# The weight sums of layer 1's modulation and of both gates, moved from the vector engine to GpSimd

## The chip, the cores and the metric

One core of one Trainium2 chip. The metric is the device time of one execution in microseconds (us), the median of the runs of one kernel. The engines are named as in the profile: PE (TensorE), DVE (VectorE), ACT (ScalarE), POOL (GpSimd) and SP (SyncE, which here issues every DMA).

## The reference, cut to what matters

Two layers of a diffusion backbone over 256 latent and 256 context tokens of width 2048. Each layer is modulated by a vector that comes from the conditioning vector `c`:

```python
silu_c = jax.nn.silu(c)
for l in range(DEPTH):
    mod_l = silu_c @ w_mod[l] + b_mod[l]
    sh_l, sc_l, gt_l = jnp.split(mod_l[:, None, :], 3, axis=-1)
    h_lat = rms_norm(x, g_pre[l]) * (1.0 + sc_l) + sh_l
    ...
    x = x + gt_l * rms_norm(y_lat, g_post[l])
```

Layer 0 is differential attention beside a two-way gated linear recurrence (HGRN2); layer 1 is a pooling mixer. `w_mod[l]` is 2048 x 6144 in float32. The change touches the products `silu_c @ w_mod` that make `sh_l` and `sc_l` of layer 1 and the gates `gt_l` of both layers: 16 blocks of 512 output columns, each a sum over 2048 rows.

## The kernel before, in words

Every large matrix product runs in float32r with both factors split in a high and a low part. A weight piece is 256 rows by 512 columns (`load_w`, line 209): one DMA of 512 KB into a tile `w` (4 buffers), ACT rounds it to `hi` (line 217), DVE forms `lo = w - hi` (line 218), and PE multiplies (line 288): 12 products of 128x512 for a group of two token tiles, 24 for a group of four. `Group.weights` (line 269) asks for a piece with raised priority, and `group` (line 433) walks over the 8 pieces of a group.

The 16 blocks of the change are made beside these groups by `gemv_row` (line 336), a generator that a `Filler` steps (line 393; `beside`, line 427, steps it some fraction of a time per piece). A step loads 256 rows of `w_mod` by 512 columns into a tile `wf`, of which there are two buffers (line 340), and adds its two k-tiles of 128 rows to the accumulator `ga` of 128x512, each scaled by a value of `csil` per partition. There are 8 steps to a block, 128 in all. When a block is done, `feature_sink` or `gate_sink` sums `ga` over the 128 partitions with products by ones on PE (lines 363 and 384) and adds bias and gain. Seven blocks are stepped in the first attention batch and the second HGRN2 batch (`hg_batch(1, ..., fills=FH)` with FH = 2, two steps per piece), five in the second attention batch and up to the layer's end, four in layer 1 (lines 1062 to 1063).

The order is set by a scheduler at build time: it simulates the engines, picks by priority, and writes one fixed program per engine. The sums stand with a lowered priority (`FILLB = -400`), their DMAs do not. At run time each engine and each queue goes through its own list in order; a wait holds everything behind it. All loads are in SP's one list, so a load that waits for its buffer holds the loads behind it.

POOL has 35 instructions in the profile before, all at the start or small: `memset`s of one column for the scans of HGRN2 (lines 576 and 579) and of a table `ct` of 48 columns (line 631), which DVE reads next.

Of the kernel before, what the change touches and what calls it, by code (L numbers as in the profile page):

```python
# [31 lines left out]
ALU = mybir.AluOpType  # L32
# [22 lines left out]
def hybrid_kernel(  # L55
# [5 lines left out]
    nc = tc.nc  # L61
# [6 lines left out]
    def alloc(tag, shape, dtype, bufs):  # L68
        return sb.tile(shape, dtype, tag=tag, bufs=bufs, name=f"{tag}_{next(names)}")

    def t2(shape, dtype=F32):
        return alloc("t2", shape, dtype, 4)
# [22 lines left out]
    def log_exp_table(after=None):  # L95
# [15 lines left out]
        out=sel, in_=ident.rearrange("p (a b) -> p b a", b=32)[:, 0:2, :], axis=AX.X)  # L111
# [97 lines left out]
    def load_w(src, k2, col, tag="w", bufs=4):  # L209
        w = alloc(tag, [P, 2, 512], F32, bufs)  # L210
        nc.sync.dma_start(
            out=w, in_=src[k2 * 256:k2 * 256 + 256, col:col + 512].rearrange("(k p) n -> p k n", p=P))
        return w
# [122 lines left out]
    def gemv_row(l, col, sink):  # L336

        acc = alloc("ga", [P, 512], F32, 2)
        for k2 in range(8):
            w = load_w(w_mod[l], k2, col, "wf", 2)  # L340
            with tc.high_priority(offset=FILLB):
                for i in range(2):
                    sc = csil[:, 2 * k2 + i, 0:1]
                    if k2 + i == 0:
                        nc.vector.tensor_scalar(out=acc, in0=w[:, i, :], scalar1=sc, scalar2=None, op0=ALU.mult)
                    else:
                        nc.vector.scalar_tensor_tensor(out=acc, in0=w[:, i, :], scalar=sc, in1=acc, op0=ALU.mult,  # L347
                                                       op1=ALU.add)
            if k2 < 7:
                yield  # L350
        fill.later.append([WAIT, lambda: sink(acc)])
        yield
# [170 lines left out]
    for i, n in ((3, 4), (7, 1)):  # L523
        t = t2([P, n, P])
# [364 lines left out]
    for f in range(4):  # L889
        fill.add(gemv_row(1, 2048 + 512 * f, feature_sink(1, 1, 4 * f, 4)))  # L890
    for f in range(3):
        fill.add(gemv_row(1, 512 * f, feature_sink(1, 0, 4 * f, 4)))
    da_batch(0, BD0, FD0)
    hg_batch(1, bgs=BH, fills=FH)
    for f in range(4):
        fill.add(gemv_row(0, 4096 + 512 * f, gate_sink(0, f)))
# [112 lines left out]
    for f in range(4):  # L1009
        t = alloc("gk", [P, 2, 512], F32, 4)  # L1010
# [54 lines left out]
    for j in range(4):  # L1065
# [12 lines left out]
        t = alloc("y", [P, 2, 512], F32, 4)  # L1078
# [115 lines left out]
```

## Time and profile before

| | |
|---|---|
| time, median of 3 runs | 1260.59 us (1259.58 to 1264.09) |
| the profiled execution's own time | 1258.11 us |
| its span in the profile | 1256.3 us |
| mean granted TensorE clock | 0.996 |
| PE busy | 1200.7 us (96%) |
| DVE busy | 897.4 us (71%) |
| ACT busy | 600.6 us (48%) |
| POOL busy | 4.4 us (0%) |
| HBM read | 260.33 MB, 209 GB/s over the span |

The span runs from the first to the last instruction; the execution's own time has some 2 us around it. Busy shares are means over stages that differ: what a change is worth in a stage is read from that stage's rows. The chain of waits follows the end of the program back from releaser to releaser, so a line in it was, at that moment, what everything else waited for. Line numbers are those of the kernel before; the change has one line less, so that a line below 347 has its number there less one.

### The profile page before, as it was taken

What the parts mean: (1) busy time and instruction counts of PE and PEld (TensorE: products, weight loads), DVE (VectorE), ACT (ScalarE), POOL (GpSimd) and SP (SyncE); (2) the same over time, 40 slices, a digit from 0 to 9 for tenths busy, and PEclk for the clock granted to TensorE, in tenths of its full rate; (3) what the DMA queues carried; (4) which work ended last, traced back from release to release, by engine and by line L of the source; (5) the groups of instructions that cost most, each with busy time, mean ns of one, the idle gap of its engine ahead of it and who ended that gap; (6) DMA issues with size and microseconds to landing.
All of it is one profiled execution on the core that took longest, in us unless ns stands there. A gap on an engine that the chain in (4) does not pass through costs nothing.

```text
span 1256.3 us, 16359 instructions
## 1 busy us (share of the span) xinstructions
PE 1200.7 (96%) x5938; PEld 951.4 (76%) x5938; DVE 897.4 (71%) x1530; ACT 600.6 (48%) x1039; POOL 4.4 (0%) x35
## 2 busy tenths in 40 slices
PE   3999999999999999999999999999999999999997
PEld 2566677778887777887787877787877877888885
DVE  3554559998767676788968697696676776976654
ACT  4231324784445633336544457764565444444452
POOL 0000000000000000000000000000000000000000
PEclk9999999999999999999999999999999999999999
DMA  9988757762453466777535266676656888875553
GB/s 290 333 303 304 264 174 234 222 197 68 137 162 99 126 220 222 250 257 228 161 101 169 84 219 223 195 250 203 218 184 202 311 303 301 268 222 185 184 209 110
DMA packets 144246, 263.52 MB, mean 210 GB/s; under 512 B 8306, under 2 KB 21540, under 8 KB 144164
## 3 DMA queue, kind: packets, MB, share of 16 engines
q1 hardware_dynamic: 144164, 262.46, 63.2%
q8 instruction: 47, 0.77, 0.2%
q14 instruction: 35, 0.29, 0.1%
HBM read 260.33 MB, written 2.10 MB: 209 GB/s over the span
## 4 chain that ended last, share of the span: by engine, by line
PE 59%; DVE 17%; DMA 16%; issue 4%; ACT 2%; SPq 1%; DVEq 0%; ACTq 0%
PE acc L288 41%; DMA wf<-in_w_mod_dram 13%; PE auxb L288 8%; DVE ga L347 5%; DVE lo L218 5%; PE aux L328 2%; PE auxb L733 2%; DMA w<-in_ev_w_in_dram 1%; SPq L128 1%; PE aux L841 1%; ACT hi L217 1%; PE auxb L817 1%; PE aux L363 1%; PE auxb L1103 1%; DVE tb L610 1%
## 5 line engine op out<-in xcount | busy, mean ns | idle before, releaser
L288 PE MATMUL acc<-hi,h 128*128 128x512 f32 x1928 | 623.8, 397 | 3.0 <-ACT h L217 2.0
L217 ACT ACTIVATE hi<-w 128x1024 fp32r<-128x1024 f32 x265 | 280.6, 1059 | 398.4 <-PE acc L288 255.0
L288 PEld LDWEIGHTS acc<-hi,h 128*128 128x128 f32 x1928 | 361.1, 188 | 86.5 <-issue 10.0
L218 DVE TENSOR_TENSOR lo<-w,hi 128x1024 fp32r<-128x1024 f32 x265 | 322.8, 1221 | 139.1 <-ACT hi L217 136.6
L288 PE MATMUL acc<-lo,h 128*128 128x512 f32 x964 | 380.9, 395 | 3.4 <-DVE lo L218 3.3
L347 DVE SCALAR_TENSOR_TENSOR ga<-wf,csil,ga 128x512 f32<-128x512 f32 x240 | 179.5, 748 | 64.0 <-DMA wf<-in_w_mod_dram 60.8
L288 PEld LDWEIGHTS acc<-lo,h 128*128 128x128 f32 x964 | 181.7, 188 | 46.7 <-DVE lo L218 7.6
L288 PE MATMUL acc<-h,hi 128*128 128x512 f32 x512 | 162.0, 397 | 0.0
L288 PEld LDWEIGHTS acc<-h,hi 128*128 128x128 f32 x512 | 95.4, 190 | 18.8 <-ACT qT L560 0.2
L288 PE MATMUL acc<-h,lo 128*128 128x512 f32 x256 | 100.8, 394 | 0.0
L288 PE MATMUL auxb<-h,hi 128*128 128x512 f32 x256 | 82.8, 405 | 0.7 <-ACT hi L217 0.4
L288 PEld LDWEIGHTS auxb<-h,hi 128*128 128x128 f32 x256 | 45.9, 188 | 24.7 <-issue 8.8
L310 DVE TENSOR_TENSOR tb<-auxb,tb 128x512 f32<-128x512 f32 x56 | 38.1, 687 | 25.9 <-PE auxb L288 25.5
L288 PEld LDWEIGHTS acc<-h,lo 128*128 128x128 f32 x256 | 48.4, 189 | 10.2
L288 PE MATMUL auxb<-h,lo 128*128 128x512 f32 x128 | 49.9, 395 | 0.0
L328 PE MATMUL aux<-h,tb 128*32 128x128 f32 (+2 forms) x320 | 29.7, 472 | 9.3 <-DMA h<-in_w_mod_dram 5.4
L218 DVE TENSOR_TENSOR h<-t,h 128x512 fp32r<-128x512 f32 x40 | 27.0, 686 | 5.7 <-ACT h L217 5.6
L819 DVE TENSOR_REDUCE tinyb<-auxb 128x1 f32<-128x512 f32 x32 | 20.7, 684 | 13.7 <-PE auxb L817 13.7
L733 PEld LDWEIGHTS auxb<-tb 128*128 128x128 f32 x192 | 25.3, 191 | 5.5 <-DVE tb L664 2.3
L733 PE MATMUL auxb<-tb 128*128 128x128 f32 x192 | 27.1, 279 | 1.5 <-DVE tb L664 1.5
L217 ACT ACTIVATE h<-t 128x512 fp32r<-128x512 f32 x40 | 24.5, 625 | 6.8 <-DVE t L912 5.0
L288 PEld LDWEIGHTS auxb<-h,lo 128*128 128x128 f32 x128 | 23.9, 188 | 4.9
(248 smaller groups left out, 1181.7 us busy)
## 6 DMA issues: line engine op xcount, KB each, us to landing
w<-in_ev_w_in_dram SPq DMA_DIRECT2D x144, 512.0 KB, 4.3
wf<-in_w_mod_dram SPq DMA_DIRECT2D x132, 512.0 KB, 4.5
w<-in_od_w_in_dram SPq DMA_DIRECT2D x64, 512.0 KB, 4.6
h<-in_w_mod_dram SPq DMA_DIRECT2D x20, 1024.0 KB, 6.9
w<-in_ev_w_out_dram SPq DMA_DIRECT2D x32, 512.0 KB, 3.7
w<-in_od_w_out_dram SPq DMA_DIRECT2D x32, 512.0 KB, 3.5
v<-in_w_mod_dram SPq DMA_DIRECT2D x24, 256.0 KB, 3.5
h<-in_w_mod_dram SPq DMA_DIRECT2D x8, 512.0 KB, 7.1
```

The lines of the kernel that those rows point to most:

```text
L128: nc.sync.dma_start(out=w[:, k:k + m, :], in_=w_mod[l][(kt0 + k) * P:(kt0 + k + m) * P, col:col + n].rearrange("(k p) n -> p k n", p=P))
L217: return (nc.scalar.activation(out=hi, in_=src, func=AF.Copy), nc.vector.tensor_tensor(out=lo, in0=src, in1=hi.bitcast(F32), op=ALU.subtract))
L218: nc.vector.tensor_tensor(out=lo, in0=src, in1=hi.bitcast(F32), op=ALU.subtract))
L288: newest[:] = [nc.tensor.matmul(self.ps[j], a, b, start=self.mm[j] == 1, stop=self.mm[j] == 6 * of)]
L310: nc.vector.tensor_tensor(out=t, in0=ps, in1=t, op=ALU.add)
L328: nc.tensor.matmul(ps[32 * j:32 * j + 32, :], cpad[:, kt, :], w[:, i, :], start=kt < 4, stop=kt >= 12)
L347: nc.vector.scalar_tensor_tensor(out=acc, in0=w[:, i, :], scalar=sc, in1=acc, op0=ALU.mult, op1=ALU.add)
L363: nc.tensor.matmul(pt[:, b, :], ev[:, sl], sel if l == 0 else ones[:, 0:2], start=True, stop=True)
L610: nc.vector.tensor_tensor_scan(out=o, data0=ones[:, 0:n], data1=src, initial=0.0, op0=ALU.mult, op1=ALU.add)
L733: nc.tensor.matmul(pt[:, i, s, :], wk(s * P), wq(s * P), start=True, stop=True)
L817: last = nc.tensor.matmul(ps[m], qT[i][r, h, sl], ks[h][k][r, :], start=n == 0, stop=n == 2)
L819: nc.vector.reduce_max(out=mx[:, m:m + 1], in_=ps[m], axis=AX.X)
```

## The change

For each k-tile, one instruction on DVE (multiply by a scalar and add the accumulator) becomes two on POOL: a multiplication of the loaded tile in place, and an addition to `ga`. The first k-tile of a block is multiplied straight into `ga`.

```diff
             with tc.high_priority(offset=FILLB):
                 for i in range(2):
                     sc = csil[:, 2 * k2 + i, 0:1]
-                    if k2 + i == 0:
-                        nc.vector.tensor_scalar(out=acc, in0=w[:, i, :], scalar1=sc, scalar2=None, op0=ALU.mult)
-                    else:
-                        nc.vector.scalar_tensor_tensor(out=acc, in0=w[:, i, :], scalar=sc, in1=acc, op0=ALU.mult,
-                                                       op1=ALU.add)
+                    t = acc if k2 + i == 0 else w[:, i, :]
+                    nc.gpsimd.tensor_scalar(out=t, in0=w[:, i, :], scalar1=sc, scalar2=None, op0=ALU.mult)
+                    if k2 + i > 0:
+                        nc.gpsimd.tensor_tensor(out=acc, in0=acc, in1=t, op=ALU.add)
```

POOL gets 256 multiplications and 240 additions of 128x512; DVE loses 16 and 240 instructions. The scheduler writes all lists anew.

SP's list in the second HGRN2 batch, before (`w`: a weight piece; `wf`: a step of the sums):

```order
L211 DMA w_4082<-in_ev_w_in_dram 128x2x512
L211 DMA wf_4001<-in_w_mod_dram 128x2x512
L211 DMA wf_4005<-in_w_mod_dram 128x2x512
L211 DMA w_4128<-in_ev_w_in_dram 128x2x512
L211 DMA wf_4054<-in_w_mod_dram 128x2x512
L211 DMA wf_4058<-in_w_mod_dram 128x2x512
L211 DMA w_4166<-in_ev_w_in_dram 128x2x512
```

and with the change:

```order
L211 DMA w_4275<-in_ev_w_in_dram 128x2x512
L211 DMA wf_4221<-in_w_mod_dram 128x2x512
L211 DMA wf_4227<-in_w_mod_dram 128x2x512
L211 DMA wf_4263<-in_w_mod_dram 128x2x512
L211 DMA w_4317<-in_ev_w_in_dram 128x2x512
L211 DMA wf_4269<-in_w_mod_dram 128x2x512
L211 DMA wf_4305<-in_w_mod_dram 128x2x512
L211 DMA w_4365<-in_ev_w_in_dram 128x2x512
```

There are still about two `wf` loads to each weight load, and each weight load still stands behind the `wf` loads ahead of it.

DVE's list at the same place, before:

```order
L347 SCALAR_TENSOR_TENSOR ga_3881<-wf_4054,csil,ga_3881 128x512
L218 TENSOR_TENSOR lo_3953<-w_3950,hi_3952 128x1024
L347 SCALAR_TENSOR_TENSOR ga_3881<-wf_4054,csil,ga_3881 128x512
L347 SCALAR_TENSOR_TENSOR ga_3881<-wf_4058,csil,ga_3881 128x512 x2
L218 TENSOR_TENSOR lo_4012<-w_4009,hi_4011 128x1024
```

and POOL's list there with the change:

```order
L345 TENSOR_SCALAR wf_4616<-wf_4616,csil 128x512 x2
L347 TENSOR_TENSOR ga_4548<-ga_4548,wf_4616 128x512 x2
L345 TENSOR_SCALAR wf_4661<-wf_4661,csil 128x512 x2
L347 TENSOR_TENSOR ga_4548<-ga_4548,wf_4661 128x512 x2
L345 TENSOR_SCALAR wf_4667<-wf_4667,csil 128x512 x2
L575 MEMSET tb_4535 128x1
L347 TENSOR_TENSOR ga_4548<-ga_4548,wf_4667 128x512 x2
```

The sums have left DVE's list, where they stood between the `lo` instructions; on POOL they fill the list, four instructions to a `wf` tile, and the small `memset`s stand among them.

## Rows read from the trace of the kernel before

**Rows 1.** The page, part 1: busy time and share of the span.
```profile
PE 1200.7 (96%) x5938; PEld 951.4 (76%) x5938; DVE 897.4 (71%) x1530; ACT 600.6 (48%) x1039; POOL 4.4 (0%) x35
```
**Rows 2.** The page, part 4: the chain that ended last, by line.
```profile
PE acc L288 41%; DMA wf<-in_w_mod_dram 13%; PE auxb L288 8%; DVE ga L347 5%; DVE lo L218 5%; PE aux L328 2%; PE auxb L733 2%; DMA w<-in_ev_w_in_dram 1%; SPq L128 1%; PE aux L841 1%; ACT hi L217 1%; PE auxb L817 1%; PE aux L363 1%; PE auxb L1103 1%; DVE tb L610 1%
```
**Rows 3.** The page, part 5: costliest groups; busy us, mean ns; idle before, releaser.
```profile
L288 PE MATMUL acc<-hi,h 128*128 128x512 f32 x1928 | 623.8, 397 | 3.0 <-ACT h L217 2.0
...
L218 DVE TENSOR_TENSOR lo<-w,hi 128x1024 fp32r<-128x1024 f32 x265 | 322.8, 1221 | 139.1 <-ACT hi L217 136.6
...
L347 DVE SCALAR_TENSOR_TENSOR ga<-wf,csil,ga 128x512 f32<-128x512 f32 x240 | 179.5, 748 | 64.0 <-DMA wf<-in_w_mod_dram 60.8
```
**Rows 4.** Busy time of each engine in four stretches, granted clock, DMA share, GB/s.
```profile
433.00:582.00 149.00, 143.90 (x684) 117.03 (x683) 111.21 (x175) 51.95 (x100) 0.69 (x7) 0.99 0.71 234
955.00:1057.00 102.00, 99.30 (x433) 78.84 (x432) 75.94 (x90) 44.81 (x50) 0.00 (x0) 1.00 0.87 298
664.00:668.00 4.00, 1.88 (x11) 1.35 (x10) 4.00 (x13) 2.68 (x6) 0.00 (x0) 1.00 0.52 157
668.00:672.00 4.00, 4.00 (x12) 3.13 (x11) 4.00 (x12) 1.93 (x4) 0.00 (x0) 0.57 0.62 202
```
**Rows 5.** Timeline of SP's queue in the second HGRN2 batch: start, us, line.
```profile
484.31 0.37 SPq L211 DMA_DIRECT2D w<-in_ev_w_in_dram  x1
484.98 1.94 SPq L211 DMA_DIRECT2D wf<-in_w_mod_dram  x2
490.97 0.37 SPq L211 DMA_DIRECT2D w<-in_ev_w_in_dram  x1
```
**Rows 6.** Instructions on tile wf, 433 to 582 us: first and last issue, landing.
```profile
L211 SPq DMA_DIRECT2D wf<-in_w_mod_dram x45: 367/368/368, 433.7 to 581.3; - x45
...
DMA to landing us min/median/max: 3.6/4.5/5.5
```
**Rows 7.** The same, 955 to 1057 us.
```profile
L211 SPq DMA_DIRECT2D wf<-in_w_mod_dram x26: 367/461/862, 955.6 to 1056.9; - x26
...
DMA to landing us min/median/max: 3.6/5.3/6.6
```
**Rows 8.** The same, issues alone: 735 to 765, 175 to 218 and 818 to 850 us.
```profile
L211 SPq DMA_DIRECT2D wf<-in_w_mod_dram x8: 367/368/368, 735.2 to 760.4; - x8
...
L211 SPq DMA_DIRECT2D wf<-in_w_mod_dram x10: 367/368/421, 175.7 to 213.7; - x10
...
L211 SPq DMA_DIRECT2D wf<-in_w_mod_dram x6: 367/368/461, 818.8 to 844.7; - x6
```
**Rows 9.** Groups of instructions on POOL, whole span.
```profile
L631 POOL MEMSET ct<- 128x48 f32 x8 | 1.1, 138 | 217.0 <-DVE tb L725 181.8 <-ACT tb L655 35.2
L576 POOL MEMSET tb<- 128x1 f32 x8 | 0.8, 100 | 379.6 <-DVE gk L559 211.6 <-ACT hi L217 140.9 <-PE aux L841 14.5
...
L196 POOL MEMSET tb<- 128x512 f32 x1 | 0.5, 524 | 0.0
...
masks.py:199 POOL TENSOR_SCALAR_AFFINE_SELECT ident<-ident 128x128 f32<-128x128 f32 x1 | 0.3, 292 | 0.0
```
**Rows 10.** The lo instruction on DVE: 433 to 582, 955 to 1057, 735 to 765 us.
```profile
L218 DVE TENSOR_TENSOR lo<-w,hi 128x1024 fp32r<-128x1024 f32 x23 | 28.1, 1220 | 6.4 <-ACT hi L217 6.4
...
L218 DVE TENSOR_TENSOR lo<-w,hi 128x1024 fp32r<-128x1024 f32 x33 | 39.6, 1218 | 0.4 <-ACT hi L217 0.3
...
L218 DVE TENSOR_TENSOR lo<-w,hi 128x1024 fp32r<-128x1024 f32 x8 | 9.7, 1217 | 0.0
```
**Rows 11.** Waits of SP's queue, 433 to 582 us: us in total, times, longest.
```profile
SPq L211 <- DVE lo L218: 50.6, 21, 5.2
SPq L211 <- DVE ga L347: 40.1, 30, 4.2
```
**Rows 12.** The chain in order of time, 640 to 680 us: start, us, what.
```profile
644.51 5.47 PE acc L288 x24
667.95 6.40 PE acc L288 x21
```

## The prediction

> **What bounds the kernel now.** Read first the busy shares: PE is busy 1200.7 of 1256.3 us, POOL not at all, DVE 71% [rows 1]. So the kernel is bound by PE, and all idle time of PE together is some 55 us, much of it at the start: no relief of another engine can give more. Then the chain of waits: it is PE's large product for 41%, but 13% of it are loads of `wf`, and 5% the sums on DVE [rows 2]. This is the sign to notice: a load that feeds a side job is in the chain, since the weight loads stand behind it in SP's one list. The timeline of SP's queue shows the pattern, one weight piece, two `wf`, one weight piece, some 6.7 us apart [rows 5], and SP's waits there name two holders, `lo` (the buffer of a weight piece, 50.6 us) and `ga` (the buffer of a `wf` tile, 40.1 us) [rows 11].
>
> That stage, 433 to 582 us, is the one to work out. 45 `wf` loads are issued in 147.6 us, 3.35 us each, 6.71 us a pair [rows 6]. With two buffers a `wf` buffer goes round in load plus sums: the median load lands 4.5 us after its issue [rows 6], two sums take 2 x 0.75 = 1.5 us [rows 3], in all 6.0, and 0.7 us are left for waiting in DVE's list. So the ring of the two buffers already runs about as fast as it can, and PE, busy 143.9 of 149 us there [rows 4], just keeps up with it.
>
> **The change part by part.**
>
> *DVE loses its sums*: 179.5 us of busy time and 64 us of waiting ahead of them [rows 3]. PE does not wait for DVE's throughput: it has 5.1 us of idle time in the first stage and 2.7 us in 955 to 1057 us [rows 4]. I count the gain as nothing; the cover is PE itself.
>
> *POOL's price for an instruction of 128x512.* No such instruction is in the trace, so it is bounded. A `memset` of 128x512 takes 524 ns, one of 128x1 100 ns: 0.83 ns a column for writing alone [rows 9]. The select on 128x128, which reads and writes one tile, takes 292 ns: (292 - 100) / 128 = 1.5 ns a column [rows 9]. So a multiplication lies between 0.52 and 100 + 512 x 1.5 = 0.87 us. A second input adds at least nothing (0.52) and, by the step from `memset` to select, once more 0.68 ns a column: 100 + 512 x 2.18 = 1.22 us. I take the upper ends, since the select is the only row in which POOL reads: a `wf` tile costs 2 x (0.87 + 1.22) = 4.2 us instead of 1.5. The lower end is 4 x 0.52 = 2.1 us, the middle 3.1.
>
> A page of the Trainium skill has prices for this: GPSIMD Engine Reference, section Performance versus the Vector engine, gives 4497 ns for an addition of 2048 float32 columns, a quarter of which is an estimate of 1.12 us, and its section Engine selection calls one input roughly line-rate, by its clock of 1.2 GHz an estimate of 0.43 us. By these a tile would take 2 x (1.12 + 0.53 with 0.1 us to start) = 3.3 us, and the sum below would come to about 1330 us. No run here shows either yet.
>
> *The second HGRN2 batch.* A buffer goes round in 4.5 + 4.2 + 0.1 for the wake-ups = 8.8 us, 4.4 us a tile; POOL alone would need 4.2. 44 intervals x 4.4 = 194 us instead of 147.6: **+46 us**. PE needs its weight pieces every 5.46 us (24 products of 228 ns, [rows 12]) and gets one in 8.8, as each stands behind two `wf` loads that wait for POOL; four `w` buffers fill once and cannot help a stage of some 22 pieces.
>
> *Layer 1, 955 to 1057 us.* 26 loads in 101.3 us, 4.05 us each, landing after 5.3 us [rows 7]. (5.3 + 4.2 + 0.1) / 2 = 4.8 us; 25 x 4.8 = 120 us: **+19 us**. PE is busy 99.3 of 102 us there [rows 4], so there is no slack to take it.
>
> *The bunches.* Elsewhere `wf` loads come in six bunches of 6 to 10, of which three stand in [rows 8]: 8 in 25.2 us, 10 in 38.0, 6 in 25.9. At 4.4 us they need 30.8, 39.6 and 22: +6, +2 and nothing. **+7 us** in all.
>
> *DVE and POOL side by side.* No row shows both reading SBUF at once. If they do so freely, this costs nothing. If one holds the other off whenever DVE reads two tiles, `lo` alone (28.1 us in the first stage, 39.6 in the second, 9.7 in the densest bunch, [rows 10]) has to find time beside POOL's sums: 45 x 4.2 + 28 = 217 instead of 194 us, 26 x 4.2 + 40 = 149 instead of 120, 34 + 10 = 44 instead of 31, together about 65 us. Nothing in the rows is nearer to either end; I take half, about **+35 us**, and keep 0 and 65.
>
> *POOL's other work.* The one-column `memset`s and the tables [rows 9] now wait in POOL's list behind up to a tile's sums, and DVE's scans, with the `lo` behind them, wait for the `memset`s. In a stage that POOL paces they are covered by its own pace; outside it a wait is up to 4 us for a few of the 24. Not in the sum, up to 15 us in the range.
>
> *PE's clock.* PE will stand still some 3 us between pieces. At 664 to 668 us PE is busy 1.88 of 4 us, and in the next 4 us its granted clock is 0.57, the half level for most of it [rows 4]; 21 products then take 6.40 us where 4.8 is usual [rows 12], 1.6 us lost. In the paced stages 5.5 + 1.6 us is still under 8.8, so this costs nothing there.
>
> *Sum*: 46 + 19 + 7 + 35 = 107 us on the profiled execution's 1258.1 us: 1365 us. That execution was 2.5 us under the median, so I say **1368 us**.
>
> **The rivals.**
>
> *B, the two engines take turns fully.* The mechanism is that of the term of which I took half. It gives 46 + 19 + 7 + 65 = 137 us, 1395 us, and with DVE's other two-input work and the `memset` waits, which then meet a busy POOL everywhere, up to 1450; I put it at 1410. For it: DVE's chain of `lo` is dense just where POOL is. Against it: nothing in the trace. The rule stands in the Trainium skill, SBUF — State Buffer, section Who interferes with whom: a DVE instruction with two SBUF inputs contends with a GpSimd instruction that reads SBUF, and the second waits to the end. No run here has shown it yet.
>
> *C, POOL is cheap.* With the middle price of 3.1 us and no interference the first stage takes 44 x 3.85 = 169 us (+22), the second 25 x 4.25 = 106 (+5): 1285 to 1300 us. For it: writing runs at 0.83 ns a column, and reading may run beside it. Against it: the select's 1.5 ns.
>
> *D, faster.* The place is the first stage: as long as load plus sums stays under the 6.71 us a pair of now, so a tile under 2.2 us or 0.55 us an instruction, the ring turns as before, DVE no longer stands in front of `lo` for a `wf` that has not landed (60.8 us of its idle time end on such a load, [rows 3]), and PE's 5.1 and 2.7 us of idle time come back: about 1250 us. It needs every POOL instruction at the price of a bare `memset`, 0.52 us, additions too.
>
> *E, no difference*: the same with the gain eaten up, 1254 to 1267 us.
>
> **How the numbers follow.** The forecast 0.50, B 0.24, C 0.18, D 0.04, E 0.04. A measurement of this kernel can tell about 0.5% (6 us) from no change. Forecast, B and C are all slower by more: slower 0.92, same 0.04, faster 0.04. The range must leave out D, E and the ends of the rest: from C's lower end, 1285, to B's upper, 1450.
>
> **What would show it.** In the profile after: POOL busy about 515 us (256 x 0.87 + 240 x 1.22); multiplications near 0.87 and additions near 1.22 us; `wf` loads in the second HGRN2 batch 4.4 to 5.2 us apart; SP's waits there led by POOL's `ga`; PE busy well under 80% of that stage, its waits ending on `hi` and `lo` whose loads came late; DVE busy near 710 us. If `lo` still takes 1.22 us and POOL's spacing is its own duration, the engines do not hold each other off; if either stretches where they meet, B holds. Wrong would be: `wf` loads still 3.4 us apart, or a PE stage that is longer while POOL stands idle for long, which would mean that the list's order and not POOL's pace is the cause.

## The result, and the profile after

The change makes the kernel slower by a fifth: 1529.54 us (median of 4 runs, 1526.01 to 1531.81) against 1260.09 us of the kernel before on the same chip, a ratio of 1.214 with a 95% interval of 1.211 to 1.216. The forecast was 1368 us, its range 1285 to 1450. The direction was right; the size and the range were not.

The page's part 1 and the chain of waits of the profiled execution (1531.81 us), which answer to [rows 1] and [rows 2]:

```profile
PE 1263.8 (83%) x5938; PEld 987.4 (65%) x5938; DVE 833.1 (54%) x1274; ACT 596.9 (39%) x1037; POOL 801.2 (52%) x531
...
POOL 43%; PE 41%; DMA 6%; DVE 5%; issue 3%; ACT 2%; SPq 1%; DVEq 0%; POOLq 0%; ACTq 0%
PE acc L288 27%; POOL wf L345 23%; POOL ga L347 18%; PE auxb L288 5%; DMA wf<-in_w_mod_dram 2%; PE aux L328 2%; DMA w<-in_ev_w_in_dram 2%; POOL ga L345 2%; PE auxb L732 1%; DVE lo L218 1%; DMA h<-in_w_mod_dram 1%; ACT hi L217 1%; PE aux L840 1%; PE auxb L816 1%; PE aux L362 1%
```

PE does the same 5938 products, but now fills 83% of a longer span. DVE lost its sums and is busy 64 us less; POOL went from 4.4 to 801.2 us and is the first name in the chain, 43%, at two lines: the multiplication (345) and the addition (347). The costliest groups, which answer to [rows 3] (line, engine, operation, tiles; busy us, mean ns; idle before and its releaser):

```profile
L345 POOL TENSOR_SCALAR wf<-wf,csil 128x512 f32<-128x512 f32 x240 | 444.6, 1863 | 23.6 <-DMA wf<-in_w_mod_dram 23.6
...
L218 DVE TENSOR_TENSOR lo<-w,hi 128x1024 fp32r<-128x1024 f32 x265 | 350.9, 1327 | 384.8 <-ACT hi L217 380.2 <-PE auxb L732 3.5
L347 POOL TENSOR_TENSOR ga<-ga,wf 128x512 f32<-128x512 f32 x240 | 330.4, 1377 | 10.5
```

The multiplication, one input and one scalar, takes 1863 ns on average, more than the addition with two inputs (1377). And `lo` on DVE, which the change does not touch, went from 1221 to 1327 ns. The instructions on the tile `wf` from 480 to 757 us, the second HGRN2 batch and the first products behind it, which answer to [rows 6] (count: ns min/median/max, first and last start):

```profile
L347 POOL TENSOR_TENSOR ga<-ga,wf x89: 1253/1280/2294, 479.8 to 755.1; 128x512 f32<-128x512 f32 x89
L345 POOL TENSOR_SCALAR wf<-wf,csil x88: 1557/1564/2818, 483.5 to 756.4; 128x512 f32<-128x512 f32 x88
L211 SPq DMA_DIRECT2D wf<-in_w_mod_dram x48: 367/368/368, 479.7 to 756.4; - x48
```

48 loads in 276.7 us, one each 5.89 us where it was 3.35. The medians of POOL's four instructions to a step add up to 2 x (1564 + 1280) = 5.69 us: POOL works without a gap, and the spacing is its own. SP's list shows who holds the loads, which answers to [rows 11], here over the whole span (us in all, times, longest):

```profile
SPq L211 <- POOL ga L347: 612.4, 117, 8.4
SPq L211 <- DVE lo L218: 273.3, 112, 7.5
```

POOL's `ga` leads, with 612 us. The loads of the weight pieces stand in the same list, and PE runs dry. Busy time of PE, PEld, DVE, ACT and POOL in that batch, then the granted clock, DMA share and GB/s, which answer to [rows 4]:

```profile
464.00:615.00 151.00, 116.70 (x527) 92.89 (x525) 48.05 (x64) 42.10 (x80) 135.21 (x90) 0.89 0.41 126
615.00:724.00 109.00, 52.50 (x215) 42.03 (x216) 29.29 (x35) 18.06 (x36) 107.61 (x77) 0.72 0.43 135
```

In the second stretch PE is busy 52.5 of 109 us at a granted clock of 0.72, POOL 107.6. The waits in that stretch show a second way by which POOL reaches PE:

```profile
DVE tb L580 <- POOL tb L575: 70.8, 4, 28.4
...
PE auxb L593 <- ACT tb L590: 30.0, 2, 20.3
...
PE auxb L588 <- ACT tb L581: 18.9, 1, 18.9
```

A `memset` of one column (line 575), which itself takes 0.1 us, stands in POOL's list behind the sums. The subtraction behind a scan of HGRN2 on DVE (line 580) waits up to 28.4 us for it, ACT for the subtraction, and PE for ACT.

Stage by stage, from the timeline of ACT (a stage ends with the last copy of its products out of PSUM). Three columns belong to runs that are told of below:

| us in the stage | before | changed | writes, packed | writes, spread | POOL, spread | DVE, spread |
|---|---|---|---|---|---|---|
| start to q of the first attention batch | 275.3 | 309.5 | 271.9 | 273.9 | 284.4 | 274.1 |
| its v and k | 111.9 | 122.1 | 111.2 | 112.9 | 134.4 | 115.0 |
| second HGRN2 batch | 191.3 | 292.4 | 338.0 | 186.2 | 207.5 | 187.7 |
| second attention batch | 144.7 | 178.2 | 138.7 | 140.3 | 174.6 | 143.2 |
| gates of layer 0 | 122.6 | 150.7 | 117.0 | 117.1 | 126.3 | 131.0 |
| end of layer 0, first z group | 125.0 | 125.6 | 126.5 | 124.7 | 127.4 | 122.7 |
| other z groups of layer 1 | 65.3 | 101.0 | 65.3 | 64.4 | 80.6 | 63.7 |
| u groups | 117.2 | 147.1 | 114.2 | 117.4 | 140.3 | 116.4 |

The changed kernel loses 101 us in the second HGRN2 batch, 34 and 28 in the two stages after it, 34 at the start, 66 in layer 1, and nothing where hardly any sums stand (end of layer 0, where POOL is busy 16.7 us).

### The profile page after: what moved, and what is told of

Same layout as the page of the kernel before. It is cut to its first block, busy times and chain, and to the rows that moved or that the text cites. A ratio compares the mean times of both kernels' runs of the same rounds, so it can differ in the third digit from the quotient of the medians.

```text
span 1529.6 us, 16553 instructions
## 1 busy us (share of the span) xinstructions
PE 1263.8 (83%) x5938; PEld 987.4 (65%) x5938; DVE 833.1 (54%) x1274; ACT 596.9 (39%) x1037; POOL 801.2 (52%) x531
## 4 chain that ended last, share of the span: by engine, by line
POOL 43%; PE 41%; DMA 6%; DVE 5%; issue 3%; ACT 2%; SPq 1%; DVEq 0%; POOLq 0%; ACTq 0%
PE acc L288 27%; POOL wf L345 23%; POOL ga L347 18%; PE auxb L288 5%; DMA wf<-in_w_mod_dram 2%; PE aux L328 2%; DMA w<-in_ev_w_in_dram 2%; POOL ga L345 2%; PE auxb L732 1%; DVE lo L218 1%; DMA h<-in_w_mod_dram 1%; ACT hi L217 1%; PE aux L840 1%; PE auxb L816 1%; PE aux L362 1%
## 5 line engine op out<-in xcount | busy, mean ns | idle before, releaser
L288 PE MATMUL acc<-hi,h 128*128 128x512 f32 x1928 | 643.6, 407 | 31.2 <-ACT hi L217 29.2
L218 DVE TENSOR_TENSOR lo<-w,hi 128x1024 fp32r<-128x1024 f32 x265 | 350.9, 1327 | 384.8 <-ACT hi L217 380.2
L217 ACT ACTIVATE hi<-w 128x1024 fp32r<-128x1024 f32 x265 | 279.3, 1057 | 518.7 <-PE acc L288 176.0
L345 POOL TENSOR_SCALAR wf<-wf,csil 128x512 f32<-128x512 f32 x240 | 444.6, 1863 | 23.6 <-DMA wf<-in_w_mod_dram 23.6
L288 PEld LDWEIGHTS acc<-hi,h 128*128 128x128 f32 x1928 | 372.1, 194 | 123.3 <-ACT hi L217 35.8
L288 PE MATMUL acc<-lo,h 128*128 128x512 f32 x964 | 391.0, 406 | 16.1 <-DVE lo L218 16.1
L347 POOL TENSOR_TENSOR ga<-ga,wf 128x512 f32<-128x512 f32 x240 | 330.4, 1377 | 10.5
L345 POOL TENSOR_SCALAR ga<-wf,csil 128x512 f32<-128x512 f32 x16 | 28.7, 1795 | 451.8 <-DVE t L490 180.1
L288 PE MATMUL acc<-h,hi 128*128 128x512 f32 x512 | 173.0, 420 | 25.8 <-ACT qT L559 19.0
L580 DVE TENSOR_TENSOR tb<-tb 128x256 f32<-128x256 f32 x16 | 8.9, 558 | 111.0 <-POOL tb L575 82.1
L588 PE MATMUL auxb<-ident,tb 128*128 128x128 f32 x32 | 7.7, 328 | 60.5 <-ACT tb L581 60.4
```

The lines of the kernel that those rows point to most:

```text
L217: return (nc.scalar.activation(out=hi, in_=src, func=AF.Copy), nc.vector.tensor_tensor(out=lo, in0=src, in1=hi.bitcast(F32), op=ALU.subtract))
L218: nc.vector.tensor_tensor(out=lo, in0=src, in1=hi.bitcast(F32), op=ALU.subtract))
L288: newest[:] = [nc.tensor.matmul(self.ps[j], a, b, start=self.mm[j] == 1, stop=self.mm[j] == 6 * of)]
L345: nc.gpsimd.tensor_scalar(out=t, in0=w[:, i, :], scalar1=sc, scalar2=None, op0=ALU.mult)
L347: nc.gpsimd.tensor_tensor(out=acc, in0=acc, in1=t, op=ALU.add)
L588: nc.tensor.transpose(pt[:, tt, :], e[:, 0, tt * P:tt * P + P], ident)
```

## The experiments

All ratios are to the kernel before, measured beside the run on the same chip (1257.7 to 1265.6 us).

**Prices by themselves** (`e1_prices`). Stretches of 16 equal instructions, nothing of the model:

```diff
+    for _ in range(16):
+        pl.tensor_scalar(out=pool, in0=pool, scalar1=sc, scalar2=None, op0=ALU.mult)
+        ve.tensor_tensor(out=lo, in0=w, in1=hi.bitcast(F32), op=ALU.subtract)
```

> This kernel leaves the whole model out: it holds only stretches of 16 equal instructions on tiles of 128x512 (lo: 128x1024), first POOL or DVE alone, then both side by side. Theory 1 (the price is POOL's own): the multiplication by a per-partition scalar takes 1.56 us and the addition 1.27 us with nothing beside them. Rival (the price in the changed kernel is waiting on other engines): alone they take 0.87 and 1.22 us or less, the upper ends that the prediction took. What in the multiplication is dear: if it is the scalar read from a tile, the same with an immediate scalar takes 0.9 us or less, and so does a copy; if it is the operation itself, the immediate takes 1.56 us too. Theory 2 (the engines hold each other off): beside DVE's lo (two inputs) the multiplication takes 1.9 us or more and lo 1.4 us or more; beside DVE's one-input multiplication and beside ACT's copy both keep their own prices. Rival: all pairs keep their own prices within 5%.

Measured, groups by line (lines 139/140, 143/144, 147/148, 151/152, 155/156 and 159/160 are pairs on two engines; some instructions of one stretch were queued into the next one, and of some pairs one engine ran alone for a time, so the means of pairs mix several cases):

```profile
L139 POOL TENSOR_SCALAR pool<-pool,sc 128x512 f32<-128x512 f32 x16 | 31.7, 1979 | 44.4 <-DVE other L95 43.0
L147 POOL TENSOR_SCALAR pool<-pool,sc 128x512 f32<-128x512 f32 x16 | 28.8, 1800 | 12.4 <-DVE pool L95 11.9
...
L144 DVE TENSOR_TENSOR lo<-w,hi 128x1024 fp32r<-128x1024 f32 x16 | 26.2, 1639 | 0.4
L143 POOL TENSOR_TENSOR ga<-ga,other 128x512 f32<-128x512 f32 x16 | 26.2, 1639 | 8.2 <-DVE ga L95 7.0
L106 POOL TENSOR_SCALAR pool<-pool,sc 128x512 f32<-128x512 f32 x16 | 25.0, 1562 | 2.0 <-DVE pool L95 0.6
...
L109 POOL TENSOR_SCALAR pool<-pool 128x512 f32<-128x512 f32 x16 | 23.8, 1488 | 1.8 <-DVE pool L95 0.5
...
L118 POOL TENSOR_TENSOR ga<-ga,other 128x512 f32<-128x512 f32 x16 | 20.1, 1258 | 0.2 <-DVE wide L95 0.2
L127 DVE TENSOR_TENSOR lo<-w,hi 128x1024 fp32r<-128x1024 f32 x16 | 19.6, 1224 | 0.4
L160 DVE TENSOR_TENSOR lo<-w,hi 128x1024 fp32r<-128x1024 f32 x16 | 19.6, 1224 | 0.4
L140 DVE TENSOR_TENSOR lo<-w,hi 128x1024 fp32r<-128x1024 f32 x16 | 19.4, 1214 | 0.1
L156 ACT ACTIVATE ev<-w 128x1024 f32<-128x1024 f32 x16 | 16.9, 1057 | 329.6 <-DVE ev L95 329.1
L115 POOL TENSOR_TENSOR pool<-pool,sc 128x512 f32<-128x512 f32 x16 | 16.6, 1037 | 0.5 <-DVE pool L95 0.5
L148 DVE TENSOR_SCALAR one<-one,sc 128x1024 f32<-128x1024 f32 x16 | 16.5, 1030 | 0.2
...
L136 DVE SCALAR_TENSOR_TENSOR dve<-one,sc,dve 128x512 f32<-128x512 f32 x16 | 16.1, 1004 | 0.0
L130 DVE TENSOR_SCALAR one<-one,sc 128x1024 f32<-128x1024 f32 x16 | 12.0, 752 | 0.0
L103 POOL COPY pool<-other 128x512 f32<-128x512 f32 x16 | 9.8, 615 | 1.4 <-POOL other L100 0.5
...
L159 POOL MEMSET other<- 128x512 f32 x16 | 8.4, 524 | 3.3 <-DVE other L95 2.4
```

Alone, the multiplication takes 1562 ns (line 106), with an immediate scalar 1488 (109), the addition 1258 (118). So the price is POOL's own, and lies in the operation: a copy takes 615 (103), and the multiplication written with two inputs, the scalar's column broadcast, 1037 (115). Side by side, addition and `lo` are both stretched to a mean of 1639 (143, 144; `lo` alone 1224, line 127). That mean mixes 7 instructions on each engine that were held with 9 that were not; in the timeline the held ones take 2.1 to 2.2 us each, and one pair comes every 2.2 us, little less than the 2.48 of the two alone: the engines nearly take turns.

POOL's multiplication goes to 1979 (139), 2137 where DVE ran beside it all the time. `lo` keeps its 1214 there (140), against the 1.4 us or more that I had expected by theory 2; the two-input instruction of the stretch before, which stood between the `lo`s, goes from 748 to 1172 (136, mean 1004). DVE's one-input multiplication goes from 752 (130) to at most 1056 beside POOL's multiplication, and to between 1.6 and 1.8 us where POOL's addition held it (the stretches of 148, mean 1030, and 152), also against what I had expected. ACT keeps its 1057 (156), and a `memset` of POOL beside `lo` leaves both alone: 524 and 1224 (159, 160). How one holds the other is seen in the timeline: two equal one-column additions on DVE, 0.15 and 1.25 us, then four `lo`s, and beside them POOL's additions.

```profile
245.47 0.15 DVE L95 TENSOR_TENSOR one<-key 128x1 f32<-128x1 f32 x1
245.54 1.25 DVE L95 TENSOR_TENSOR dve<-key 128x1 f32<-128x1 f32 x1
...
249.24 8.76 DVE L144 TENSOR_TENSOR lo<-w,hi 128x1024 fp32r<-128x1024 f32 x4
```
```profile
245.50 11.42 POOL L143 TENSOR_TENSOR ga<-ga,other 128x512 f32<-128x512 f32 x6 [7.02 <-DVE ga L95]
```

The second one-column addition ended at 246.79 us, 1.29 us after POOL's first addition had begun, and an addition alone takes 1.26: DVE stood until it was over. Beside POOL's other instructions the longest of these one-column additions took 0.60 us (multiplication by a scalar, of 1.56) and 0.92 (multiplication by a broadcast column, of 1.04). So POOL's two-input instructions held DVE for nearly the whole of their time, and the multiplication by a scalar for little more than a third of its own. The Trainium skill states this rule in SBUF — State Buffer, section Who interferes with whom: DVE instructions with two SBUF inputs, or in a mode that uses both ports, and POOL instructions that read SBUF lock each other out for a whole instruction, while a POOL instruction that only writes takes no part against a two-input one. This run agrees for the addition (1.25 us) and for the `memset`, which holds nothing. It does not for POOL's multiplication by a scalar: `lo` kept its price beside it, and two of DVE's multiplications (0.75 us each alone) fitted into each 2.1 us of one of POOL's (1.56 alone). There the measurement decides.

**Three ways to loosen POOL's hold**, each on the changed kernel.

```diff
@@ e2_mult_on_dve
-                    nc.gpsimd.tensor_scalar(out=t, in0=w[:, i, :], scalar1=sc, scalar2=None, op0=ALU.mult)
+                    nc.vector.tensor_scalar(out=t, in0=w[:, i, :], scalar1=sc, scalar2=None, op0=ALU.mult)
@@ e3_own_queue
-            w = load_w(w_mod[l], k2, col, "wf", 2)
+            w = load_w(w_mod[l], k2, col, "wf", 2, nc.gpsimd)
@@ e4_spread
-FH, FG, FO, FD0, FD1, FZ, FU = 2, .5, .5, .7, .7, .5, .5
+FH, FG, FO, FD0, FD1, FZ, FU = 1, .75, .5, .9, .9, .5, .5
```

> The multiplications go to DVE, the additions stay on POOL. Theory 1 (POOL's price paces the wf ring): POOL's tile falls from 5.66 to 2 x 1.27 = 2.5 us; a buffer then goes round in load 3.9 to 4.5 + one multiplication 0.48 (the 16 plain multiplications of the kernel before) + two additions 2.5 + about 0.7 of waiting = 7.6 to 8.2, 3.8 to 4.1 us a tile instead of 3.35, so the second HGRN2 batch costs 20 to 35 us more than before and the whole 1290 to 1340 us; POOL busy 305 to 340 us. Rival (DVE and POOL holding each other off is the main cost, whatever POOL's share): DVE has more work again, additions stretch to 1.7 us or more, 1400 us or more.

Measured 1389.24 us (ratio 1.104, 1.098 to 1.109): between the two. POOL is busy only 387 us, and still more than half of the loss stays. POOL's addition takes 1595 ns on average and `lo` 1454.

> All as in the changed kernel, but the wf loads are issued from POOL's queue instead of SP's. Theory 3 (POOL's pace reaches PE because SP's one list holds the weight loads behind wf loads): the weight loads run free, SP's waits on POOL's ga (612 us in the changed kernel) are gone, PE works at its own pace between the places where a finished sum is consumed, and the time falls to 1300 to 1420 us, although POOL's busy time stays 700 to 800 us. Rival (PE waits for the sums themselves, where they are consumed): the waits go to the matrix products by ones that sum ga, and the time stays above 1480 us.

Measured 1512.79 us (1.202, 1.193 to 1.211): a miss for theory 3. SP no longer waits for `ga`, but PE's products that consume a finished sum do:

```profile
PE aux L362 <- POOL ga L347: 73.7, 3, 29.5
```

and the subtractions behind the scans waited longer for the `memset` of line 575 than in the changed kernel (98 against 82 us). POOL is late all the same, and the place where PE meets it moved. The run is no clean test of theory 3, though: an issue of a load takes POOL 763 ns here, 98 us for the 128 of them, which lengthens the very step that the run was to hide.

> Sums spread more evenly: one step per piece instead of two in the HGRN2 batches (FH = 1), more in the attention batches (FG = .75, FD0 = FD1 = .9). Theory 1 with 3 (a stage is lengthened only by the steps that POOL cannot do beside it): one step per piece wants a tile every 5.5 us where POOL needs 5.7 to 6.5, so the HGRN2 batches lose little, and the time falls to 1400 to 1480 us, the rest sitting where the left-over steps are drained. Rival (POOL's total busy time sets the end, wherever it lies): 1530 us within 1%.

Measured 1482.94 us (1.178, 1.171 to 1.185), just above theory 1's range. The second HGRN2 batch fell from 292.4 to 212.2 us; but the second attention batch took 193.5 and the gates 170.5 us, more than in the changed kernel: the steps moved, and the loss with them.

**Memsets, and both at once, and a cheaper multiplication.**

```diff
@@ e6_memsets_dve, the same at lines 578 and 630; e7 has this and the edit of e3
-                nc.gpsimd.memset(e[:, 0, T - 1:T], 0.0)
+                nc.vector.memset(e[:, 0, T - 1:T], 0.0)
@@ e8_broadcast_mult
-                    nc.gpsimd.tensor_scalar(out=t, in0=w[:, i, :], scalar1=sc, scalar2=None, op0=ALU.mult)
+                    nc.gpsimd.tensor_tensor(out=t, in0=w[:, i, :], in1=sc.to_broadcast([P, 512]), op=ALU.mult)
```

> The 24 small memsets of the scans and tables go from POOL to DVE, else the changed kernel. Theory 4 (the scans of HGRN2 wait for a one-column memset that stands in POOL's list behind a backlog of sums, and PE for the scans): the 82 us of waits of the scan for POOL vanish, PE's 60 us before the products of the scans too, and the time falls by 50 to 110 us, to 1420 to 1480 us. Rival (theory 1 with 3: the weight loads behind the wf loads set the same stages anyway): by less than 25 us, 1505 us or more.

Measured 1520.05 us (1.201, 1.195 to 1.207): theory 4 falls. The waits for the `memset`s are gone, and the same stages wait for weight pieces instead:

```profile
ACT hi L217 <- DMA w<-in_ev_w_in_dram: 255.0, 40, 11.3
```

255 us where the changed kernel has 147.5. Beside their own measurements of the kernel before, the two kernels are 15 us apart: most of the waits for the two one-column `memset`s (82 us for line 575, 28 for 578) stood in front of other ones.

> Both at once: wf loads from POOL's queue and the small memsets on DVE, so that nothing of the main work stands behind the sums but the products by ones that consume a finished sum. If the list of SP and the memsets are together the way by which POOL's pace reaches PE: 1300 to 1400 us. Rival (what is left, PE's products that consume a finished sum, hold PE in its list just as long): 1450 us or more, with the waits of those products on ga grown from 99 us to 150 us or more.

Measured 1470.74 us (1.162, 1.155 to 1.169): the rival's time. With both ways closed, PE waits 82 us at line 362 and 33 at line 383 for sums, 115 where the rival wanted 150 or more; and as in e3 the issues on POOL take 98 us of its time. So this run doesn't tell what holds PE most.

> The multiplication is written as a two-input one with the scalar's column broadcast (1.04 us alone in the prices by themselves, instead of 1.56), else the changed kernel. Theory 1 (the price of POOL's tile sets the time): a tile falls from 5.66 to 4.6 us, POOL busy from 801 to 640 to 680 us, and of the 270 us that the change cost a part of 30 to 45 per cent goes, to 1410 to 1450 us. Rival (two inputs hold DVE off more than one): lo longer than 1.40 us on average and the time above 1480 us.

Measured 1476.48 us (1.166, 1.160 to 1.172). The tile is cheaper (POOL busy 690 us, a step each 5.10 us in the second HGRN2 batch), but `lo` takes 1449 ns on average, and DVE is busy 932 us against 833 in the changed kernel, for the same work. The time lies between the two ranges: 58 us less than the changed kernel, beside their own measurements of the kernel before, where theory 1 wanted 80 us or more.

**Writes instead of sums** (`e5_writes_only`) takes the holding off away and keeps POOL's time:

```diff
-                    nc.gpsimd.tensor_scalar(out=t, in0=w[:, i, :], scalar1=sc, scalar2=None, op0=ALU.mult)
+                    nc.gpsimd.memset(w, 0.0)
                     if k2 + i > 0:
-                        nc.gpsimd.tensor_tensor(out=acc, in0=acc, in1=t, op=ALU.add)
+                        nc.gpsimd.memset(w, 0.0)
+                        nc.gpsimd.memset(w[:, i, 0:384], 0.0)
+                    nc.gpsimd.memset(acc, 0.0)
```

> POOL keeps its time per tile but reads nothing of the SBUF: each multiplication and addition is replaced by memsets of the same loaded tile and of ga, 0.95 + 0.95 + 0.42 + 0.52 = 2.84 us per k-tile against 1.56 + 1.27 = 2.83 (the sums are left out: shift, scale and gates are then wrong numbers). In the prices by themselves a memset beside lo left both at their own durations. Theory 1 (POOL's own time is the cost, the engines' holding each other off a small addition): POOL busy about 720 us, a tile 5.7 us, lo back at 1.22 us, and the time 1440 to 1500 us, that is 30 to 90 us less than the changed kernel. Rival, theory 2 (holding each other off is the main cost): below 1400 us.

Two executions took 1264.22 and 1286.77 us; the profiled one is the first, a single execution no slower than the kernel before (1265.58), with POOL busy 681 us:

```profile
PE 1201.4 (95%) x5938; PEld 953.3 (76%) x5938; DVE 738.6 (59%) x1274; ACT 596.4 (47%) x1037; POOL 680.9 (54%) x1027
```

This looked like a clean win for theory 2, but it was not: the scheduler had also written another list. Between the same copies of ACT in the second HGRN2 batch (from the end of its q to the end of its z groups), SP issues 26 `wf` loads in 164 us, where the changed kernel has 42 in 259 us and the kernel before 44 in 158. It places steps by the durations that it assumes, and spread the memsets as it had not spread the sums. Two things had changed at once, and the next runs separate them.

**A spread and a packed list, by hand.**

```diff
@@ load_w, in e9 and e10
+        with tc.issue_after(piece[-1].ins) if tag == "wf" and piece else ExitStack():
+            dma = nc.sync.dma_start(...)
+        if tag == "w":
+            piece[:] = [dma]
@@ the steps per piece, in e9 and e10 (e10 has the multiplication of e8 too)
+FH, FG, FO, FD0, FD1, FZ, FU = {4: 0.6, 7: 1.1, 5: 1.1, 6: 1.1}, 0.5, 0.5, (0.6, 1.1), (0.6, 1.1), 0.57, 0.57
@@ e11: the memsets of e5, each w and wf load behind the one before it, and
+FH, FG, FO, FD0, FD1, FZ, FU = 3, .5, .5, .3, .7, .5, .5
```

> The sums as in the changed kernel (1.56 + 1.27 us), but SP's list is spread by hand: each wf load is queued behind the weight load of its step, and the steps per piece are set so that a step comes every 5.5 to 7 us in every stage (.6 per piece of the groups of two token tiles, 1.1 of four, in the second HGRN2 batch too; .57 in layer 1), where the changed kernel has 46 steps in the 259 us (158 us before) of the z groups. New theory 5 (a stage costs what its number of steps times POOL's tile goes over its own length; the list that the scheduler wrote packs steps as if POOL were fast): no stage has more steps than fit, and the time is 1265 to 1330 us, the rest from DVE and POOL holding each other off. Rival, theory 2 (the holding off is the main cost): POOL and DVE meet just as often, so 1400 us or more. POOL busy 720 to 820 us by both.

Measured 1384.63 us (1.100, 1.097 to 1.104): the range of neither. Beside their own measurements of the kernel before, the spread takes 143 of the 269 us away, and 127 stay.

> The same spread list, with the multiplication by a broadcast column (1.04 us alone). Theory 5: the tile is 4.6 instead of 5.66 us alone, all stages have room, and the time is 1255 to 1300 us, 0 to 30 us less than with the scalar multiplication. Theory 2: lo is held longer (1.45 us against 1.33 on average in the runs without the spread), and the time stays above 1350 us.

Measured 1412.68 us (1.123, 1.120 to 1.126), slower than with the dearer multiplication. Part 1 and the chain by engine:

```profile
PE 1246.3 (89%) x5938; PEld 981.4 (70%) x5938; DVE 998.0 (71%) x1274; ACT 598.2 (43%) x1037; POOL 729.7 (52%) x531
...
PE 53%; DVE 26%; POOL 7%; issue 6%; ACT 5%; DMA 3%; SPq 1%; DVEq 0%; ACTq 0%; POOLq 0%
```

POOL does not pace here (7% of the chain); DVE is busy 998 us (892 in e9) and has 26%. A POOL multiplication with two reading inputs costs DVE more than one with a scalar, as the 0.92 and 0.60 us of e1 say.

> POOL only writes, as in the run with memsets in place of the sums (the sums are left out), which took as long as the kernel before; but now the list of SP is packed by hand: w and wf loads in the order in which the program is written, three steps per piece in the z groups of the second HGRN2 batch (48 steps), fewer before. No engine holds another off. Theory 5: 48 steps of 5.7 us are 274 us where the two z groups had 158 us, so the time is 1350 to 1400 us, and the z groups alone take 100 to 120 us more. Rival (packing costs nothing unless the engines hold each other off): 1265 to 1290 us.

Measured 1392.14 us: as theory 5 had it. The instructions on `wf` in that batch:

```profile
L347 POOL MEMSET wf<- x86: 943/957/976, 417.0 to 664.3; 128x1024 f32 x86
...
L350 POOL MEMSET wf<- x80: 410/418/437, 419.0 to 663.5; 128x384 f32 x80
L214 SPq DMA_DIRECT2D wf<-in_w_mod_dram x43: 367/368/404, 419.5 to 663.9; - x43
```

43 loads in 244.4 us, 5.82 us each, with nobody held off (`lo` 1224 ns on average). The table's third column shows it: 147 us more in this stage than before, and no other one is over 2 us longer. A stage costs at least what its steps times POOL's step exceed its own length: by that count 48 steps were to add 116 us between the same copies of ACT, and 146 were measured.

**The kernel before with the loads on POOL's queue** (`e12_before_own_queue`; in `gemv_row`, `load_w(..., nc.gpsimd)`).

> The kernel before, its sums on DVE, with the wf loads issued from POOL's queue, which is idle there. If the wf loads in SP's list (13 per cent of the chain of the kernel before) cost PE time, it ends 5 to 20 us earlier than before, at 1240 to 1255 us. Rival (PE alone is the bound and the loads in the chain are only the way the chain was followed): 1255 to 1265 us.

Measured 1278.63 us (1.016, 1.013 to 1.018): slower than either. So the 13% of `wf` loads in the chain [rows 2] were not time to be had in this way; why it became slower stays open.

**One list for four divisions of the work.** In all four, SP's `w` and `wf` loads stand in one and the same order (that of the program text, with e9's steps per piece); the program texts differ only in the instructions that form the sums: those of the changed kernel (e13), of e5 (e14), of the kernel before (e15), of e2 (e16). In the traces of e13 and e14 PE, DVE and ACT also run the same operations on the same tiles in the same order, and POOL is busy about as long by its own prices (684 us of writes; 256 x 1.562 + 240 x 1.258 = 702 us of sums), so that apart from a few small loads these two differ only in whether POOL's instructions read SBUF or just write it. In e15 and e16 the scheduler ordered some of the other engines' work otherwise.

```diff
+        with tc.issue_after(piece[-1].ins) if piece and "wf" in (tag, piece[0]) else ExitStack():
+            dma = nc.sync.dma_start(...)
+        piece[:] = [tag, dma]
```

> Sums on POOL as in the changed kernel, the list of SP spread by hand and fixed: w and wf loads in the order in which the program is written, .6 step per piece of two token tiles, 1.1 of four, .57 in layer 1. This is the reference of the four runs with one list; as the run with the spread list before it: 1370 to 1400 us by all theories.

> The same list, POOL writes only (memsets of equal time, the sums are left out). If the list itself or POOL's own pace of 5.7 us a step is what costs: 1330 us or more. If DVE and POOL holding each other off is what costs: 1255 to 1285 us, DVE busy near 739 us and lo at 1.22 us.

> The same list, the sums on DVE in one instruction each, as in the kernel before; POOL does none. If the list itself costs: 1290 us or more. If not: 1245 to 1270 us, and below 1255 us it would beat the kernel before, since no stage has its steps in a bunch.

> The same list, multiplication on DVE and addition on POOL, so that POOL's tile is 2.5 us alone and 3.2 us with what it was stretched to before, far under the 5.5 us of a step: POOL's pace can't bound any stage. Holding off as the main cost: 1310 to 1370 us, with DVE busy above 930 us. POOL's longer tile as the main cost of the spread list: 1255 to 1300 us.

| SP's list | POOL writes only | sums on POOL | half and half | sums on DVE |
|---|---|---|---|---|
| spread, one order | 1243.41 (e14) | 1383.56 (e13) | 1354.48 (e16) | 1254.70 (e15) |
| packed | 1392.14 (e11) | 1529.54 (the change) | 1389.24 (e2) | 1260.09 (before) |

The ratios to the kernel before in the first row are 0.987 (0.984 to 0.991), 1.100 (1.096 to 1.103), 1.076 (1.072 to 1.079) and 0.996 (0.994 to 0.998). SP's lists of the second row differ from one another, the first row's don't. Sums instead of writes cost 140 us in the spread list, which is the clean comparison, and 137 in the packed ones; packing costs 149 us with writes and 146 with sums. In these runs the two costs about add up. That they do so to a few us is not shown to be more than chance, since e11 was packed by hand and more tightly (48 loads between the copies named above) than the change (42). With the writes, e14 (part 1; `lo` and two short instructions of DVE, the last with min/median/max):

```profile
PE 1194.4 (96%) x5938; PEld 949.5 (77%) x5938; DVE 739.3 (60%) x1274; ACT 596.8 (48%) x1037; POOL 684.5 (55%) x1027
...
L222 DVE TENSOR_TENSOR lo<-w,hi 128x1024 fp32r<-128x1024 f32 x265 | 324.1, 1224 | 303.4 <-ACT hi L221 293.9 <-PE auxb L736 8.3 <-DMA wf<-in_w_mod_dram 0.3
...
L667 DVE TENSOR_TENSOR tb<-tb,qT 128x256 f32<-128x256 f32 x40 | 16.7, 422 | 1.9 <-ACT tb L666 1.3
...
L831 DVE SCALAR_TENSOR_TENSOR tinyb<-tinyb,nlam,tinyb x16: 219/220/223, 397.8 to 795.3; 128x1 f32<-128x1 f32 x16
```

and with the sums, e13, the same groups and POOL's two:

```profile
PE 1235.9 (90%) x5938; PEld 974.5 (71%) x5938; DVE 896.0 (65%) x1274; ACT 597.6 (43%) x1037; POOL 863.7 (63%) x531
...
L349 POOL TENSOR_SCALAR wf<-wf,csil 128x512 f32<-128x512 f32 x240 | 478.0, 2001 | 64.7 <-DMA wf<-in_w_mod_dram 64.1 <-issue 0.6
...
L222 DVE TENSOR_TENSOR lo<-w,hi 128x1024 fp32r<-128x1024 f32 x265 | 373.4, 1413 | 277.3 <-ACT hi L221 266.1 <-DMA w<-in_ev_w_in_dram 5.7 <-PE auxb L736 4.4
...
L351 POOL TENSOR_TENSOR ga<-ga,wf 128x512 f32<-128x512 f32 x240 | 355.2, 1480 | 10.0
...
L667 DVE TENSOR_TENSOR tb<-tb,qT 128x256 f32<-128x256 f32 x40 | 29.9, 756 | 2.5 <-ACT tb L666 2.3
...
L831 DVE SCALAR_TENSOR_TENSOR tinyb<-tinyb,nlam,tinyb x16: 219/386/1077, 430.0 to 889.5; 128x1 f32<-128x1 f32 x16
```

The same DVE work takes 896 instead of 739 us: `lo` 1413 instead of 1224 ns, a product of 128x256 in the HGRN2 heads 756 instead of 422, and the 128x1 step in the middle of the attention's softmax up to 1077 instead of 220. POOL's multiplication went from 1562 alone to 2001. Both sides pay. e16, where POOL's step is short, shows what DVE's side comes to:

```profile
PE 1230.1 (91%) x5938; PEld 972.4 (72%) x5938; DVE 992.9 (73%) x1530; ACT 591.0 (44%) x1033; POOL 405.3 (30%) x275
...
PE 45%; DVE 27%; DMA 14%; issue 6%; ACT 5%; POOL 2%; SPq 1%; DVEq 0%; POOLq 0%; ACTq 0%
```

POOL has 2% of the chain and is busy 30%, and the kernel is still 100 us slower than e15. With POOL's pace out of the way most of what is left is, as far as can be told, DVE being held: it is busy 993 us, where e14's 739 and 256 multiplications at their price alone (485 ns in e1) make 863. Not all of it need be: a `wf` buffer now waits for two engines in turn, SP's waits for `ga` are 190 us against 99 in e15, and no run takes that apart. e15, the sums on DVE in the spread list, is the one version with the sums in it that beats both kernels: 1254.70 us, 0.4% less than before.

## Why the prediction was wrong, point by point

- *What bounds the kernel*: right. PE bounds it, the ring of two `wf` buffers was near its limit [rows 6], and the steps come in bunches. e15, which spreads them, is 0.4% faster.
- *POOL's price*: **here the size failed.** The upper end for the multiplication, 0.87 us, was taken from the select on 128x128 [rows 9]; it takes 1.56 us alone. The addition was right (1.22 forecast, 1.26). A tile costs 5.64 us and not 4.2, and that changes the bound too: 5.64 is more than half the ring's 4.5 + 5.64 us, so that POOL itself paces the stage, and not load plus sums. With 5.64 us the prediction's own terms give 44 x 5.64 - 147.6 = +101 (instead of +46) in the second HGRN2 batch, 25 x 5.64 - 101.3 = +40 (+19) in layer 1, and +29 (+7) in the three bunches shown: 170 instead of 72 us, 98 of the 161 us that were missing. Measured: +101 in the HGRN2 batch, +66 in layer 1, +107 in the other stages of the table. That the first agrees to the microsecond is luck (e11 gave 146 where such a count gave 116); what the others lost beyond this is not POOL's price alone. The Trainium skill's price for one input in GPSIMD Engine Reference, section Engine selection, roughly line-rate, an estimate of 0.43 us, was farther off; nearest to it came the copy, 0.615.
- *DVE and POOL side by side*: **the second failure.** I took +35 with bounds of 0 and 65, counting `lo` alone, in three stages, as added time on POOL. In one list (e13 against e14) it costs 140 us. It can't be carried over whole to the changed kernel's list, for 170 and 140 make 310, and the change cost 269. What the bounds left out: other DVE instructions with two SBUF inputs are held too, down to a step of 128x1 in the softmax, also where POOL is not the pace (e16), and POOL's own instructions stretch. Rival B had the mechanism, and by its test (`lo` stretches where they meet) it holds; its 1410 us and its 1450 went with the wrong tile.
- *Memsets behind POOL*, not in the sum, up to 15 us: right in the sum. A single wait is longer than the 4 us forecast, up to 28.4, and all of line 575's come to 82 us, but e6 gives back only some 15.
- *DVE's relief counted as nothing*: nearly. From e15 to e14, where the sums leave DVE and nobody is held off, it is 11 us, part of which may come from the other engines' changed order.
- *PE's clock, 0*: the granted clock fell to 0.72 where PE starved, and PE was busy 63 us more in all. That is where POOL paces and PE has time, so little of it can count; no run takes it apart.
- *Rivals*: C and D needed a cheap tile, E no effect; none came true. That the list's order could be a cause was named only as what would make the prediction wrong ("PE longer while POOL stands idle"). It was a cause while POOL was busy: the steps are packed into stages that POOL can't serve. The packing was there before the change too, and was harmless at DVE's 1.5 us a tile.

What stays open: how the 140 us divide between DVE's delays and POOL's stretched step when both are there (e16 puts the first near 100 us, with a shorter POOL share and the way through two engines in it), and what the clock adds.

## What to carry to other kernels

Before moving side work to an idle engine, time its instructions alone, form by form, and then beside the other engine's: the same product cost 1.56 us in one form and 1.04 in another, and the price from "a similar row" was off by almost two. Then compare that price times the number of steps with the length of each stage, for a list that was fitted to a fast engine packs them so that a slow one can't keep up. And on this chip POOL and DVE are not two engines while both read SBUF: count every two-input DVE instruction that runs beside POOL's, short ones in chains too; in the spread list a cheaper POOL instruction with two inputs made it worse. Last, a mean over a stretch where two engines only partly ran side by side hides the price: 1639 ns was in truth 2166 when held and 1224 when not.

## What the runs showed of the hardware that I had not expected

- POOL's multiplication by a scalar over 128x512 takes 1562 ns, with an immediate 1488, while a two-input product with a broadcast column takes 1037, an addition 1258, a copy 615, a `memset` 524 to 578.
- An instruction of one column on DVE (0.15 us) can take 1.25 us when POOL's addition holds it, and at most 0.60 beside POOL's multiplication by a scalar, though that one takes longer itself (1.56 against 1.26 us). The price of a POOL instruction and what it costs DVE are two numbers.
- A load issued from POOL's list took 725 to 763 ns of POOL's time (e12, e3).
- A long wait in the list of waits may be worth nothing: 110 us of waits for two `memset`s were removed for about 15 us.
